# Two layer norms as pipelines of four stages in a fixed order, with other products between their last transposes

## The chip, the cores and the metric

The kernel runs on one core of a Trainium2 chip. The metric is the device time of one execution in microseconds. A core has five engines with queues of their own: TensorE (PE; its weight loads are PEld), VectorE (DVE), ScalarE (ACT), GpSimd (POOL) and SyncE (SP). Each engine takes its instructions in a fixed order and waits on semaphores for what others make. TensorE reads SBUF and writes banks of PSUM.

## The reference

One layer of a streaming encoder on 1024 frames of 1024 features, all in float32:

```
h = LN1(ALPHA * x + 0.5 * swiglu(x, ffn1_w1, ffn1_w3, ffn1_w2))
proj = h @ w_in                      # RWKV-7 time mixing, latent attention, two gates
mix  = (g_rwkv * y_rwkv + g_mla * y_mla) @ w_o
h = LN2(ALPHA * h + mix)
h = LN3(ALPHA * h + 0.5 * swiglu(h, ffn2_w1, ffn2_w3, ffn2_w2))

def layer_norm(x, g, b):
    mu = mean(x); var = mean((x - mu) ** 2)
    return (x - mu) * rsqrt(var + 1e-5) * g + b
swiglu(x, w1, w3, w2) = (silu(x @ w1) * (x @ w3)) @ w2
```

## The kernel before

Frames lie in eight tiles of 128 rows. Every matrix product is made of three products of a high and a low part (`mm3`, lines 240 to 243), so an operand is split into `h` and `l` first (`hilo`, line 250: the high part by ScalarE, the rest by VectorE or GpSimd at line 247; `split`, lines 1204 to 1210).

`ffn` (line 629) runs a feed-forward part. Weights come in pairs of tiles, and a pair is done by a Strassen-like scheme: seven products of sums of weight blocks with sums of blocks of x. `w_a` and `w_s` (lines 396 and 408) load weights and make the sums `rs`, `rt` and their parts `sh`, `sl`, `th`, `tl`; `XOps` (line 271) makes the blocks `b11`, `b21`, `b22` and the sums `t1` to `t4` of x. `Start` (line 429) handles the first three pairs; their first products (`p1`, `p2`) need no sums of weights.

`block` (line 568) makes the product that ends each of the three parts, in groups of rows of the second matrix: for every group all eight tiles get their products and are added into `acc` by VectorE. In the last group `ln_tile` (line 660) follows each tile: the sum over a row comes with the last addition (line 604), `nm` is the negative mean (667), ScalarE squares and sums (669), GpSimd makes the scalars `rs` and `nb` (674, 675, 684). Then the first and second norm have two ways. Tiles 0 to 5: ScalarE normalizes into `z` (685), GpSimd multiplies by the gain (686), VectorE adds the bias (687). Tiles 6 and 7, and all of the third norm: two VectorE operations (672, 678). In the first two norms the tile is then transposed by TensorE (695), eight blocks of 128x128 in two banks, and split by `sink.put` (lines 266 and 285: `HT` for the first norm, `XOps` for the second) into the operands of the next part.

The order is made by a scheduler when the program is built. It takes the instructions as written and lays each engine's queue by costs of its own; what stands in the queue then is fixed. After the first norm comes `mid` (line 1215), whose first job multiplies two tiles of `w_in` by the transposed tiles (`first`, line 1376). `BETWEEN` (line 457) says after which tile of the second norm a first product of a pair may come.

Buffers come in rings: `wraw` has 4 for raw weights, `wsp` 6 and `wsp2` 8 for split ones, `xp` 4 and `xf` 3 large ones; eight banks of PSUM are shared in four rings of two.

## Time and profile before

| | us |
|---|---|
| median of 3 runs (lowest, highest) | 2444.42 (2440.49, 2445.41) |
| profiled execution, its own time | 2448.22 |
| its span in the trace | 2446.3 |
| TensorE busy | 2317.0 (95%) |
| VectorE busy | 1503.5 (61%) |
| ScalarE busy | 797.6 (33%) |
| GpSimd busy | 649.2 (27%) |

The profiled execution's time is its span and 1.9 us around it. Busy times of matmuls overlap by their pipeline: one is shown 0.39 us long at the high clock, and the next starts 0.23 us after it. In the rows, an arrow in brackets gives how long an engine had been idle before an instruction and what released it. "PEclk" is the share of full clock that TensorE was granted in a stretch.

### The profile page before, as it was taken

To read this page: it belongs to the slowest core of one execution; us is meant where nothing else is said; L and a number is where in the kernel's file an instruction comes from. 1 tells how busy PE (TensorE), PEld (TensorE's weight loads), DVE (VectorE), ACT (ScalarE), POOL (GpSimd) and SP (SyncE) were. 2 spreads that over 40 slices of the span, in tenths; PEclk is the share of its full clock that TensorE was granted. 3 is DMA by queue.
4 is the path that set the end of the run, shared out by engine and by line. 5 is a ranking of instruction groups with operands and counts; after the bars stand their busy time and mean duration, and the time that the engine had idled before them with its cause. 6 is when DMAs were issued, how large, how long until landed. Compare 5 with 4: busy or idle time off the path is not lost.

```text
span 2446.3 us, 32472 instructions
## 1 busy us (share of the span) xinstructions
PE 2317.0 (95%) x12670; PEld 1902.9 (78%) x12670; DVE 1503.5 (61%) x2328; ACT 797.6 (33%) x1183; POOL 649.2 (27%) x559
## 2 busy tenths in 40 slices
PE   9999999999989998999999799889689999999998
PEld 7888888888768777877777588767468888888886
DVE  7866655666536546445373667766696666556666
ACT  5332223211353222222222566732442222231111
POOL 1322223322412003030122533343532222232311
PEclk9999999999989999999989999999799999999999
DMA  5322224532123313225226744463132222245311
GB/s 177 117 86 86 87 78 146 195 104 63 72 97 123 95 70 95 70 82 138 73 91 218 256 130 119 160 229 113 69 107 92 91 82 86 78 152 180 112 39 69
DMA packets 106265, 276.71 MB, mean 113 GB/s; under 512 B 36408, under 2 KB 36536, under 8 KB 106112
## 3 DMA queue, kind: packets, MB, share of 16 engines
q1 hardware_dynamic: 72912, 200.63, 24.1%
q0 software_dynamic: 19824, 71.38, 9.4%
q10 hardware_dynamic: 13376, 2.62, 0.7%
q8 instruction: 100, 1.64, 0.3%
q14 instruction: 53, 0.43, 0.1%
HBM read 193.98 MB, written 80.61 MB: 112 GB/s over the span
## 4 chain that ended last, share of the span: by engine, by line
PE 77%; DVE 7%; DMA 6%; issue 3%; POOL 3%; ACT 3%; SPq 0%; ACTq 0%; DVEq 0%; POOLq 0%
PE pd L241 5%; PE pd L242 5%; PE pd L243 5%; PE bb L242 4%; PE bb L241 4%; PE bb L243 4%; PE ba L241 4%; PE ba L242 4%; PE ba L243 4%; PE bc L243 4%; PE bc L242 4%; PE bc L241 4%; PE bd L243 4%; PE bd L242 4%; PE bd L241 4%
## 5 line engine op out<-in xcount | busy, mean ns | idle before, releaser
L241 PE MATMUL pd<-xh,wh 128*128 128x512 f32 x576 | 237.8, 413 | 1.7 <-DVE xl L1208 1.7
L242 PE MATMUL pd<-xl,wh 128*128 128x512 f32 x576 | 227.7, 395 | 0.0
L243 PE MATMUL pd<-xh,wl 128*128 128x512 f32 x576 | 227.5, 395 | 0.0
L247 POOL TENSOR_TENSOR la<-ra,ha 128x1024 fp32r<-128x1024 f32 x40 | 98.2, 2455 | 331.8 <-ACT ha L251 331.5
L241 PEld LDWEIGHTS pd<-xh,wh 128*128 128x128 f32 x576 | 109.9, 191 | 28.0 <-DVE xl L1208 1.9
L243 PEld LDWEIGHTS pd<-xh,wl 128*128 128x128 f32 x576 | 110.0, 191 | 24.4
L242 PEld LDWEIGHTS pd<-xl,wh 128*128 128x128 f32 x576 | 110.1, 191 | 21.6 <-issue 1.0
L251 ACT CAST ha<-ra 128x1024 fp32r<-128x1024 f32 (+1 forms) x45 | 46.4, 1033 | 245.4 <-PE bb L242 61.2
L247 POOL TENSOR_TENSOR fx<-raw,fx 128x1024 fp32r<-128x1024 f32 (+1 forms) x24 | 64.3, 2693 | 202.6 <-ACT fx L251 190.9
L247 POOL TENSOR_TENSOR wl<-raw,wh 128x1024 fp32r<-128x1024 f32 x28 | 73.0, 2610 | 140.1 <-ACT wh L251 121.5
L251 ACT CAST fx<-raw 128x1024 fp32r<-128x1024 f32 x44 | 44.1, 1049 | 158.2 <-DVE acc L607 47.6
L247 DVE TENSOR_TENSOR tl<-rt,th 128x1024 fp32r<-128x1024 f32 x41 | 85.5, 2086 | 0.0
L225 ACT CAST wh<-raw 128x1024 fp32r<-128x1024 f32 x36 | 37.7, 1048 | 145.9 <-PE pd L242 84.7
L247 POOL TENSOR_TENSOR hb<-rb,hb 128x512 fp32r<-128x512 f32 x41 | 56.9, 1387 | 85.8 <-ACT hb L251 85.7
L226 DVE TENSOR_TENSOR wl<-raw,wh 128x1024 fp32r<-128x1024 f32 x36 | 46.4, 1288 | 48.2 <-ACT wh L225 39.3
L222 POOL DMA_DIRECT2D raw<-in_w_in_dram x36 | 19.8, 550 | 201.1 <-DVE wl L226 80.7
L1666 ACT ACTIVATE pe<-s,anm,qs 128x512 f32<-128x512 f32 (+2 forms) x96 | 63.9, 670 | 25.2 <-DVE anm L1660 12.3
L607 DVE TENSOR_TENSOR acc<-acc,bd 128x512 f32<-128x512 f32 x72 | 49.3, 684 | 35.1 <-PE bd L243 34.9
L607 DVE TENSOR_TENSOR acc<-acc,ba 128x512 f32<-128x512 f32 x72 | 49.3, 684 | 34.9 <-PE ba L243 34.9
L1672 POOL TENSOR_SCALAR pe<-pe,asum 128x128 f32<-128x128 f32 (+3 forms) x64 | 47.7, 747 | 82.5 <-DVE asum L1671 76.7
L607 DVE TENSOR_TENSOR acc<-acc,bc 128x512 f32<-128x512 f32 x72 | 49.2, 684 | 32.2 <-PE bc L243 32.2
L607 DVE TENSOR_TENSOR acc<-acc,bb 128x512 f32<-128x512 f32 x72 | 49.2, 684 | 31.6 <-PE bb L243 31.4
(671 smaller groups left out, 6981.0 us busy)
## 6 DMA issues: line engine op xcount, KB each, us to landing
ra<-in_ffn_w_dram POOLq DMA_DIRECT2D x49, 512.0 KB, 3.7
raw<-in_ffn_w_dram SPq DMA_DIRECT2D x44, 512.0 KB, 4.2
raw<-gd_ffn SPq DMA_DIRECT2D x42, 512.0 KB, 4.4
rb<-in_ffn_w_dram POOLq DMA_DIRECT2D x41, 512.0 KB, 4.6
gd_ffn<-g SPq DMA_DIRECT2D x41, 512.0 KB, 2.6
raw<-in_w_in_dram POOLq DMA_DIRECT2D x36, 512.0 KB, 3.8
h<-acc SPq DMA_DIRECT2D x16, 512.0 KB, 2.6
gates<-dt SPq DMA_DIRECT2D x16, 512.0 KB, 3.3
```

The costliest lines, as they stand in the source:

```text
L222: (nc.gpsimd if K.pq else nc.sync).dma_start(out=raw[:rows, :n], in_=src)
L225: nc.scalar.copy(out=hi[:rows, :n], in_=raw[:rows, :n])
L226: nc.vector.tensor_tensor(out=lo[:rows, :n], in0=raw[:rows, :n], in1=hi[:rows, :n].bitcast(F32), op=ALU.subtract)
L241: nc.tensor.matmul(out, lhsT=lh, rhs=rh, start=start, stop=False)
L242: nc.tensor.matmul(out, lhsT=lh, rhs=rl, start=False, stop=False)
L243: nc.tensor.matmul(out, lhsT=ll, rhs=rh, start=False, stop=stop)
L247: eng.tensor_tensor(out=out, in0=a, in1=b, op=ALU.subtract)
L251: K.nc.scalar.copy(out=hi, in_=raw)
L607: nc.vector.tensor_tensor(out=at[:, ns], in0=at[:, ns], in1=ps, op=ALU.add)
L1666: nc.scalar.activation(out=pe[:, b:b + w], in_=s[:, 0:w], func=AF.Exp, scale=qs, bias=nm, accum_out=sm2[:, i:i + 1])
L1672: nc.gpsimd.tensor_scalar(out=pe[:, 0:n], in0=pe[:, 0:n], scalar1=sm_, scalar2=1.0, op0=ALU.mult, op1=ALU.mult)
```

## The change

In the first and second norm the last group becomes a loop of eleven steps inside a region in which the scheduler leaves TensorE, VectorE and GpSimd in the order in which the code is written. Step t makes the products and scalars of tile t, the gain of tile t-1 on GpSimd, the bias of tile t-2 on VectorE, and the transposes of tile t-3. All tiles go this way, in place in `acc`. After steps 8 and 9 of the first norm stand the first halves of the two products of `first`, whose weights are now loaded by SyncE's queue before the norm (class `Pre`); their results wait in two `raw` buffers. In the second norm two of the six first products stand after each of the steps 7, 8 and 9, then the sums of the first pair's weights, whose raw tiles are loaded earlier; the last sums of x (`X.end`) and those of the second pair come after the last subtraction of `put`. The last feed-forward part gets other groups: nine pairs and a last group of four. The third norm keeps its way.

```diff
@@ block
-        if final:
-            ln_tile(K, t, at, su, gb, sink, emit_h)
-            if between:
-                between(t)
+            hooks.weights()
+            sink.begin()
+            junk = K.tmp.tile([P, D], F32, name="junk", tag="r", bufs=2)
+            E = mybir.EngineType
+            with K.tc.manual_schedule(engines={E.PE, E.DVE, E.Pool}):
+                for t in range(NT + 3):
+                    if t < NT:
+                        ln_norm(K, at(t), last(t, at(t), ops), junk)
+                    if 1 <= t <= NT:
+                        nc.gpsimd.tensor_tensor(out=at(t - 1), in0=at(t - 1), in1=gb[0], op=ALU.mult)
+                    if 2 <= t < NT + 2:
+                        ln_out(K, t - 2, at(t - 2), gb, emit_h)
+                    if t >= 3:
+                        turn(K, t - 3, at(t - 3), sink)
+                    hooks.step(t)
@@ new functions
+def ln_norm(K, y, su, junk):
+    nc = K.nc
+    nm = ln_mean(K, su)
+    rs = ln_scale(K, y, nm, junk)
+    nb = K.small.tile([P, 1], F32, name="nb")
+    nc.gpsimd.tensor_tensor(out=nb, in0=rs, in1=nm, op=ALU.mult)
+    nc.scalar.activation(out=y, in_=y, func=AF.Identity, scale=rs, bias=nb)
+def ln_out(K, t, y, gb, emit_h):
+    K.nc.vector.tensor_tensor(out=y, in0=y, in1=gb[1], op=ALU.add)
+    emit_h(t, y, slice(0, D))
+class Pre:
+    def weights(self):
+        K = self.K
+        self.w = [load_w(K, K.a["w_in"][i]) for i in range(2)]
+        self.raw = [rawtile(K, "pre") for _ in range(2)]
+    def step(self, t):
+        if t not in (NT, NT + 1):
+            return
...
+            mm3(K.nc, ps, w[0][:, ks], w[1][:, ks], xs[k][0][:, 0:HALF], xs[k][1][:, 0:HALF], k == 0, k == KT - 1)
+        K.nc.scalar.copy(out=self.raw[i][:, 0:HALF], in_=ps)
@@ Start
+        if not self.w0:
+            self.raws = [w_raw(self.K, self.w13, self.first, n) for n in ("ra", "rb")]
...
+        if t == NT + 1:
+            self.sums(self.first, *self.raws)
...
+        with self.K.tc.issue_after(self.X.last.ins):
+            self.X.end()
+            self.sums(self.first + 1)
-BETWEEN = (0, 0, 0, 0, 1, 1, 1, 0)
+BETWEEN = (0, 0, 0, 0, 0, 0, 0, 2, 2, 2, 0)
@@ groups
-GROUPS = [(2 * i, 2 * i + 1) for i in range(8)] + [(16, 17, 18), (19, 20, 21)]
+_PAIRS = [(2 * i, 2 * i + 1) for i in range(9)]
+GROUPS = (_PAIRS[:8] + [(16, 17, 18), (19, 20, 21)], _PAIRS + [(18, 19, 20, 21)])
@@ mid
-    fill.add([lambda: load_w(K, a["w_in"][0]), lambda: load_w(K, a["w_in"][1])], first)
+    def first():
+        for w, raw, consume in zip(K.pre.w, K.pre.raw, (c_wa, c_g0)):
+            ps = K.pd.tile([P, S], F32, name="pd", tag="pd")
...
+            nc.scalar.copy(out=raw[:, HALF:S], in_=ps[:, HALF:S])
+            consume(raw)
```

What this does to the queues, at the three places where it matters. TensorE's queue at the end of the first norm, before (`ident,acc` is a group of four transposes, `fx` and `wh,gh` are operands of the last group, `xh,wh` of `first`):

```order
L695 MATMUL bd<-ident,acc 128x128 x4
L695 MATMUL ba<-ident,acc 128x128 x4
L596 MATMUL bc<-fx 128x512
L597 MATMUL bc<-fx 128x512
L695 MATMUL bd<-ident,acc 128x128 x4
L695 MATMUL ba<-ident,acc 128x128 x4
...
L241 MATMUL pd<-xh,wh 128x512
L242 MATMUL pd<-xl,wh 128x512
L243 MATMUL pd<-xh,wl 128x512
```

and in the changed kernel, where the rows left out are the rest of the 24 products after each tile:

```order
L749 MATMUL bd<-ident,acc 128x128 x4
L749 MATMUL ba<-ident,acc 128x128 x4
L242 MATMUL bb<-xh,wh 128x512
L243 MATMUL bb<-xl,wh 128x512
L244 MATMUL bb<-xh,wl 128x512
...
L749 MATMUL bc<-ident,acc 128x128 x4
L749 MATMUL bd<-ident,acc 128x128 x4
L242 MATMUL ba<-xh,wh 128x512
...
L749 MATMUL bb<-ident,acc 128x128 x4
L749 MATMUL bc<-ident,acc 128x128 x4
```

Before, the last four tiles were transposed one after another with no product between; now 24 products stand after each of tiles 5 and 6, and tile 7 comes last.

GpSimd's queue in the second norm, before (`rs` and `nb` are a tile's scalars, `z<-z,lngb` is the gain, `la` and `t` are splits):

```order
L247 TENSOR_TENSOR t_14352<-r_14354,t_14352 128x4x128
L674 TENSOR_SCALAR rs<-sq 128x1
L675 TENSOR_TENSOR rs<-rs,neghalf 128x1
L684 TENSOR_TENSOR nb<-rs,nm 128x1
L686 TENSOR_TENSOR z<-z,lngb 128x1024
L247 TENSOR_TENSOR t_14352<-r_14427,t_14352 128x4x128
```

and in the changed kernel:

```order
L248 TENSOR_TENSOR la<-ra,ha 128x1024
L710 TENSOR_SCALAR rs<-sq 128x1
L711 TENSOR_TENSOR rs<-rs,neghalf 128x1
L720 TENSOR_TENSOR nb<-rs,nm 128x1
L632 TENSOR_TENSOR acc<-acc,lngb 128x1024
L710 TENSOR_SCALAR rs<-sq 128x1
L711 TENSOR_TENSOR rs<-rs,neghalf 128x1
L720 TENSOR_TENSOR nb<-rs,nm 128x1
L632 TENSOR_TENSOR acc<-acc,lngb 128x1024
L248 TENSOR_TENSOR t_14445<-r_14447,t_14445 128x4x128
L632 TENSOR_TENSOR acc<-acc,lngb 128x1024
```

Before, a tile's gain stood right behind its own scalars; now the gain behind a tile's scalars is that of the tile before.

VectorE's queue at the end of the second norm, before (`t_14363` is the low part of `t2`, `t_14135` that of `t3`, `r_14591` belongs to `t4`, `s_` are sums of first products):

```order
L247 TENSOR_TENSOR tl<-rt,th 128x1024
L247 TENSOR_TENSOR r_14578<-bd,r_14569 128x512
L247 TENSOR_TENSOR r_14568<-bd,r_14568 128x512
L485 TENSOR_TENSOR s_14637<-cp,ba 128x512
L485 TENSOR_TENSOR s_14653<-cp,bb 128x512
L485 TENSOR_TENSOR s_14669<-cp,bc 128x512
L247 TENSOR_TENSOR t_14363<-r_14578,t_14363 128x4x128
L247 TENSOR_TENSOR r_14591<-b_14133,t_14363 128x1024
L247 TENSOR_TENSOR r_14597<-b_14133,t_14363 128x1024
L247 TENSOR_TENSOR b_14134<-bd,b_14134 128x4x128
L247 TENSOR_TENSOR t_14135<-r_14568,t_14135 128x4x128
```

and in the changed kernel:

```order
L423 TENSOR_TENSOR rs<-rb 128x512
L248 TENSOR_TENSOR rs<-rs,ra 128x512
L248 TENSOR_TENSOR rt<-ra,rb 128x512
L248 TENSOR_TENSOR rt<-ra,rs 128x512
L248 TENSOR_TENSOR sl<-rs,sh 128x1024
L248 TENSOR_TENSOR tl<-rt,th 128x1024
L248 TENSOR_TENSOR r_14641<-bd,b_14142 128x512
...
L248 TENSOR_TENSOR t_14145<-r_14640,t_14145 128x4x128
L314 TENSOR_TENSOR t_14456<-r_14650,t_14456 128x4x128
L248 TENSOR_TENSOR r_14664<-b_14143,t_14456 128x1024
```

Before, the sums of the first two pairs were mixed with the splits of the tiles; now the first pair's stand just ahead of the splits of tile 7, and the second pair's come after them. From the end of the first norm's products to the second norm TensorE's queue holds the same products in the same order in both.

## Rows read from the trace of the kernel before

**Rows 1.** Busy time by engine in two stretches; then clock, DMA share, GB/s.
```profile
633.80:697.50 63.70, 49.94 (x231) 41.20 (x230) 36.64 (x69) 28.82 (x44) 30.20 (x39) 0.87 0.19 71
1701.60:1805.20 103.60, 69.51 (x272) 53.64 (x273) 79.79 (x116) 47.88 (x72) 52.03 (x48) 0.82 0.26 92
```
**Rows 2.** Timeline of TensorE, first norm: start, duration, instruction, idle before.
```profile
633.87 0.39 PE L241 MATMUL bb<-wh,gh 128*128 128x512 f32 x1
...
651.11 0.60 PE L695 MATMUL bd<-ident,acc 128*128 128x128 f32 x4
651.54 0.60 PE L695 MATMUL ba<-ident,acc 128*128 128x128 f32 x4
...
678.68 1.09 PE L695 MATMUL bd<-ident,acc 128*128 128x128 f32 x4 [6.74 <-DVE acc L687]
...
686.31 0.80 PE L241 MATMUL pd<-xh,wh 128*128 128x512 f32 x1 [1.68 <-DVE xl L1208]
...
691.60 0.63 PE L241 MATMUL pd<-xh,wh 128*128 128x512 f32 x1
...
692.39 0.39 PE L243 MATMUL pd<-xh,wl 128*128 128x512 f32 x1
692.62 0.39 PE L241 MATMUL pd<-xh,wh 128*128 128x512 f32 x1
```
**Rows 3.** Timeline of TensorE, second norm and the start of the next part.
```profile
1742.99 1.09 PE L695 MATMUL bd<-ident,acc 128*128 128x128 f32 x4 [6.71 <-DVE acc L687]
...
1766.07 1.12 PE L695 MATMUL ba<-ident,acc 128*128 128x128 f32 x4 [8.77 <-DVE acc L687]
...
1805.26 0.39 PE L242 MATMUL bd<-t,sh 128*128 128x512 f32 x1
```
**Rows 4.** Timeline of all engines, the first tile of the first norm.
```profile
637.70 0.69 DVE L604 SCALAR_TENSOR_TENSOR acc<-acc,bc 128x512 f32<-128x512 f32 x1 [1.12 <-PE bc L597]
...
640.01 0.19 POOL L674 TENSOR_SCALAR rs<-sq 128x1 f32<-128x1 f32 x1 [24.04 <-ACT z L669]
...
641.15 1.24 ACT L685 ACTIVATE z<-acc,nb,rs 128x1024 f32<-128x1024 f32 x1 [1.23 <-POOL nb L684]
...
642.47 2.40 POOL L686 TENSOR_TENSOR z<-z,lngb 128x1024 f32<-128x1024 f32 x1 [1.36 <-ACT z L685]
```
**Rows 5.** Timelines of VectorE and GpSimd, two places of the first norm.
```profile
650.63 1.23 DVE L687 TENSOR_TENSOR acc<-z,lngb 128x1024 f32<-128x1024 f32 x1 [1.10 <-POOL z L686]
650.68 1.22 POOL L674 TENSOR_SCALAR rs<-sq 128x1 f32<-128x1 f32 x1
...
672.77 2.35 POOL L686 TENSOR_TENSOR z<-z,lngb 128x1024 f32<-128x1024 f32 x1
673.07 3.13 DVE L672 SCALAR_TENSOR_TENSOR c<-acc,nm,lngb 128x1024 f32<-128x1024 f32 x1 [0.22 <-ACT z L669]
```
**Rows 6.** Timeline of GpSimd: first of the constants' fills, then the second norm.
```profile
669.34 0.10 POOL L705 MEMSET hsel<- 128x2 f32 x1
...
1721.07 0.19 POOL L674 TENSOR_SCALAR rs<-sq 128x1 f32<-128x1 f32 x1
...
1756.49 1.29 POOL L247 TENSOR_TENSOR t<-r,t 128x512 fp32r<-128x512 f32 x1 [7.33 <-ACT t L251]
...
1774.80 2.76 POOL L247 TENSOR_TENSOR la<-ra,ha 128x1024 fp32r<-128x1024 f32 x1 [0.23 <-PE ba L242]
```
**Rows 7.** Timeline of VectorE, second norm: a short subtraction and a long one.
```profile
1793.80 0.68 DVE L247 TENSOR_TENSOR r<-bc,b 128x512 f32<-128x512 f32 x1
1794.40 1.21 DVE L247 TENSOR_TENSOR sl<-rs,sh 128x1024 fp32r<-128x1024 f32 x1
```
**Rows 8.** Timeline of TensorE and VectorE, end of the third norm.
```profile
2435.27 0.39 PE L597 MATMUL bd<-fx 128*128 128x512 f32 x1
...
2436.52 0.68 DVE L604 SCALAR_TENSOR_TENSOR acc<-acc,bd 128x512 f32<-128x512 f32 x1
...
2438.33 0.20 DVE L667 TENSOR_SCALAR nm<-su 128x1 f32<-128x1 f32 x1
...
2441.90 1.41 DVE L678 SCALAR_TENSOR_TENSOR acc<-c,rs,lngb 128x512 f32<-128x512 f32 x2 [0.71 <-POOL rs L675]
```

More of the change, by code (lines that the diff above doesn't have):

```diff
@@ L178, in body @@
                   lambda t, h, ns: nc.sync.dma_start(out=K.h2[t][:, ns], in_=h[:, ns]), X,
-                  before_last=st.weights, between=st.step)
+                  hooks=st)
             ffn(K, "ffn2", "ln3", X, st, resid=lambda t: K.h2[t],
@@ L311, in put @@
         hilo(K, self.r1, f("t1", 0), f("t1", 1), nc.gpsimd)
-        hilo(K, r2, f("t2", 0), f("t2", 1), nc.vector)
+        nc.scalar.copy(out=f("t2", 0), in_=r2)
+        self.last = nc.vector.tensor_tensor(out=f("t2", 1), in0=r2, in1=r("t2", 0), op=ALU.subtract)
     def end(self):
@@ L444, in step, with sums @@
             self.todo.pop(0)()
+        if t == NT + 1:
+            self.sums(self.first, *self.raws)
+    def sums(self, p, *raws):
+        w_s(self.K, self.w13, p, self.pairs[p].w, *raws)
     def run(self):
@@ L541, in tiles @@
         K = self.K
-        if (final and i == 2) or (not final and gi in (1, 2, 4, 6, 8)):
-            t = (K.xf if final else K.xp).tile([P, 4, S], F32R, name="fx", tag="x")
+        if (final and i >= 2) or (not final and gi in (1, 2, 4, 6, 8)):
+            t = (K.xf if final and i == 2 else K.xp).tile([P, 4, S], F32R, name="fx", tag="x")
             return [t[:, q] for q in range(4)]
@@ L565, in one, with block, mult, last @@
         return gh, None, wh, wl
-def block(K, src, groups, ln, resid, emit_h, sink, before_last=None, between=None):
+def block(K, src, groups, ln, resid, emit_h, sink, hooks=None):
     nc = K.nc
     acc = None
-    last = sink is None
+    tsl = lambda t: slice(t * P, (t + 1) * P)
+    def mult(t, ns, ops):
+        ps = bank(K)
+        for q, (gh, gl, wh, wl) in enumerate(ops):
+            st, sp = q == 0, q == len(ops) - 1
+            if gl is not None:
+                mm3(nc, ps, gh[:, tsl(t)], gl[:, tsl(t)], wh[:, ns], wl[:, ns], st, sp)
+            else:
+                nc.tensor.matmul(ps, lhsT=gh[:, tsl(t)], rhs=wh[:, ns], start=st, stop=False)
+                nc.tensor.matmul(ps, lhsT=gh[:, tsl(t)], rhs=wl[:, ns], start=False, stop=sp)
+        return ps
+    def last(t, at, ops):
+        su = K.small.tile([P, 2], F32, name="su")
+        for n, ns in halves():
+            ps = mult(t, ns, ops)
+            nc.vector.scalar_tensor_tensor(out=at[:, ns], in0=at[:, ns], scalar=1.0, in1=ps,
+                                           op0=ALU.mult, op1=ALU.add, accum_out=su[:, n:n + 1])
+        return su
     for gi, fs in enumerate(groups):
@@ L635, in ffn @@
         if nxt in st.pairs:
-            w_s(K, w13, nxt, st.pairs[nxt].w)
+            if not getattr(st.pairs[nxt], "summed", False):
+                st.sums(nxt)
         else:
@@ L675, in ln_tile @@
     nc.gpsimd.tensor_tensor(out=rs, in0=rs, in1=K.neghalf[:, 0:1], op=ALU.pow)
-    if fast:
-        for n, ns in halves():
-            nc.vector.scalar_tensor_tensor(out=y[:, ns], in0=c[:, ns], scalar=rs, in1=gb[1][:, ns],
-                                           op0=ALU.mult, op1=ALU.add)
-            if not transpose and t == NT - 1:
-                emit_h(t, y, ns)
-    else:
-        nb = sm.tile([P, 1], F32, name="nb")
-        nc.gpsimd.tensor_tensor(out=nb, in0=rs, in1=nm, op=ALU.mult)
-        nc.scalar.activation(out=z, in_=y, func=AF.Identity, scale=rs, bias=nb)
-        nc.gpsimd.tensor_tensor(out=z, in0=z, in1=gb[0], op=ALU.mult)
-        nc.vector.tensor_tensor(out=y, in0=z, in1=gb[1], op=ALU.add)
@@ L883 @@
 LAG = 2
-LNF = 6
 LA = 2
```

128 lines of the change are left out of this document (65 added, 63 removed).

## The prediction

> **What bounds the kernel now.** I read the page's busy shares first: TensorE is busy for 95% of the span, so over most of it only fewer products would help, and the change removes none. Next I cut the span at the places the diff touches. Around the first norm's last tiles, 63.7 us hold 49.94 us of TensorE work at a mean clock of 0.87; around the second norm 103.6 us hold 69.51 us at 0.82, and part of that busy time is itself stretched by the low clock [rows 1]. Everywhere else TensorE is nearly full. So the prize is what TensorE loses in these two stretches, and a little at the end.
>
> The third view is TensorE's timeline in the first of them. The last group's products start at 633.87. Then TensorE waits for normalized tiles, 6.74 us the longest time, and 1.68 us for the last split; the first product of the next section starts at 686.31, at the low clock (1.2 GHz, 0.63 us a product there), and the pace of the high one (2.4 GHz), 0.23 us from product to product, is back at 692.39 [rows 2]. In the second norm the same waits are 6.71 us and 8.77 us, and the dense stream of the next feed-forward part is there at 1805.26 [rows 3].
>
> The fourth view is one tile's way through the engines [rows 4]: VectorE adds the last product (637.70) and makes the mean, ScalarE squares, GpSimd makes the scalars from 640.01, ScalarE normalizes from 641.15, GpSimd multiplies by the gain (642.47, 2.40 us), and VectorE adds the bias. Some 9 us pass from the last product to a tile that can be transposed, against 3.63 us of products for a tile (16 of 0.227 us). The scheduler lets TensorE run out of products before these ways are over.
>
> **The change, part by part.** Eight tiles go through a fixed pipeline: at step t TensorE multiplies tile t, GpSimd makes its scalars and then multiplies tile t-1 by the gain, VectorE adds the bias to tile t-2, and TensorE transposes tile t-3. All eight tiles now take the GpSimd multiply; before, two of eight had a VectorE route. Products that need only earlier tiles stand between the last transposes: 48 in the first norm (the first half of two input projections), 72 in the second (first products of three pairs, which the scheduler had placed there partly).
>
> *The pace.* A GpSimd step is 1.11 us of scalars (640.01 to about 641.12) and 2.40 us of multiply, 3.5 us. But the trace shows that a VectorE operation with both inputs in SBUF and a GpSimd operation don't run side by side: a 0.19 us scalar takes 1.22 us beside the bias addition at 650.63, and VectorE's operation at 673.07, on as many elements as the bias addition, takes 3.13 us beside a GpSimd multiply that began at 672.77 [rows 4, 5]. Each step has one bias addition of 1.14 us (1.23 us in the row, less the overlap with the next). So I take 2.40 + 1.11 + 1.14 = 4.65 us a step. VectorE's own work in a step is 1.46 us for the additions and the mean, 1.14 us for the bias and 1.2 us for splits, 3.8 us; TensorE's is 3.63 + 0.86 us in the first norm and 2.72 + 0.86 us in the second.
> The Trainium skill ("SBUF — State Buffer", section "Who interferes with whom") calls the port pair that the two engines share an exclusive lock, so that whichever starts first blocks the other for its whole instruction; the rows just named agree. If the two merely ran beside each other, the step would be 3.5 us, and both norms would go by the first rival below.
>
> *First norm.* GpSimd's first multiply is now queued behind the second tile's scalars. Tile 1's scalars come 3.63 us after tile 0's (640.01), from 643.6 to 644.7 [rows 4]; so the multiply of tile 0 ends at 647.1, and, with tile 2's scalars held up by the first bias addition, that of tile 1 at 651.7. Four steps of 4.65 us later, at 670.3, tile 5 is multiplied, and it can be transposed at 671.5. From there TensorE has three tiles to transpose (0.86 us each, two groups of four that start 0.43 us apart in [rows 2]) and 48 products (10.9 us): 13.5 us, to 685.0. The fills of constants that stand in GpSimd's queue (669.34 to 672.77, about 3 us [rows 5, 6]) delay the last two multiplies to some 680; their transposes wait behind products anyway, so I cost them at nothing; without those products they would cost the 3 us. Then the 1.7 us for the last split, as before, and 2 us for a low clock after the wait at tile 5 (686.31 to 692.39 lost 2.9 us to it): the next products start near 689. Before, 48 products later than 686.31 is 692.39 plus the remaining 34 of 0.227 us, 700.1. Gain 11 us. Bounds: TensorE without any wait would be there at 633.87 + 128 x 0.227 + 6.9 + 10.9 + 1.7 = 682.5, a gain of 17.6 us; steps of 6.5 us would gain nothing.
> The halves computed early go through a copy by ScalarE before they are shifted, and two of four staging buffers are held until then. The copies lie beside the next 24 products, and weights loaded late have over 20 us until they are needed; I take 0, with bounds of -1 and +2 us.
>
> *Second norm.* GpSimd's first scalars are at 1721.07 [rows 6], behind two weight subtractions that stay there. Two tiles' scalars and the first multiply end at about 1725.9. Four steps bring tile 4 to 1744.5, a third weight subtraction in the queue (2.76 us) and two more steps tile 6 to 1756.6, and a split of 1.29 us with the last multiply tile 7 to 1760.3 [rows 6]. Here VectorE becomes the chain: a late tile's split is seven operations of 0.60 us [rows 7], 4.2 us, because these tiles feed the sums of a Strassen product. After the bias of tile 6 come the splits of tiles 5, 6 and 7 (12.6 us), three additions for the early products (1.8 us), the bias of tile 7 (1.14 us), the sums of the first pair's weights (4 of 0.60 and 2 of 1.21 us, 4.8 us), 20.3 us, and some 2 us of waits against GpSimd: 1782.6. TensorE has its last transposes behind it at about 1768 and then waits some 15 us, because all that is left needs tile 7. With 2 us of low clock it is dense as from 1785. Before, it was dense at 1805.26 with 16 products of that part done [rows 3], 3.6 us, which is 1801.6. The second pair's sums now stand behind the last subtraction (t4) on VectorE; they end some 15 us later, about when TensorE wants them; 1.5 us for that. Gain 15 us. Bounds: VectorE alone, never waiting, needs 49 us from the first addition, some 3 us before GpSimd's first scalars, which gives 1767 and a gain of 33 us; at the other end the wait eats all of it, 0 us or a loss as in the third rival.
>
> *Last norm.* The last group has four blocks of rows in place of three, so a tile has 22 products, 5.0 us, and VectorE, 4.3 us a tile, no longer falls behind. Now the last product starts at 2435.27 and its addition at 2436.52, the last mean follows only at 2438.33, after the tile before, and the last scaling at 2441.90 [rows 8]. Without the backlog the addition starts 0.4 us after the product does, the mean 0.7 us later, and the scaling 2.5 us after that (the way of [rows 4] up to the scalars): 2438.9. Gain 3 us, bounds 0 and 3.5.
>
> *Sum.* 11 + 15 + 3 = 29 us. The profiled execution took 2448.22 us (span 2446.3), so its like would take 2419; the runs' median is 2444.42, 3.8 us lower, so I predict 2415 us.
>
> **Rivals.** First, the queues never wait: the bias additions fit between GpSimd's operations. Then 17.6 + 33 + 3 = 54 us, 2390 us. For it: TensorE's and VectorE's own work would allow it. Against it: the blocked operations of [rows 5] are the rule when both engines are at work.
> Second, the wait only moves: in the second norm the 15 us at the end grow by what is saved between, because VectorE has the same splits and sums in any order; 11 + 0 + 3 = 14 us, 2430 us. For it: VectorE is busy 79.79 of the 103.6 us there [rows 1]. Against it: its busy time there holds blocked operations too (as the 3.13 us of [rows 5]), and those fixed queues may spare.
> Third, slower: with fixed queues one late tile holds all that is queued behind it, the stages stop overlapping, and the step grows to a tile's own way from the addition of its last product to the end of its bias addition, 8.4 us (637.70 to 644.87 and 1.23 us, [rows 4, 5]). The 29 us shrink by 12 for each us of the step (six steps in each norm), so 7.0 us a step decides; at 8.4 us it is 16 us slower, 2461 us. For it: the multiply of a tile waits for the scalars of the next. Against it: the multiply, the bias and the transposes belong to three different tiles.
> Fourth, the order changes nothing that can be measured: 2444 us. It would need steps near 7 us.
>
> **Numbers.** The forecast has 62%, its own range 2403 to 2428; the first rival 9%, the second 17%, the third 7%, the fourth 5%. The range that should hold the time 8 times in 10 takes in most of the second rival and goes part of the way to the first: 2400 to 2436. About 0.2% (4.9 us) is what a measurement can tell from no change; that gives 0.89 faster, 0.05 the same, 0.06 slower.
>
> **What would show it.** Right: in the first norm GpSimd's multiplies start 4.3 to 5 us apart, TensorE's one long wait is before the transposes of tile 5, and none stands before the last ones; in the second, TensorE waits once for 10 to 17 us after its last transposes, until VectorE's last split; at the end the last mean directly follows the last addition. Wrong: multiplies 3.5 us apart (first rival), a final wait over 25 us (second), steps of 7 us and more (third), or a loss in the sections between, where TensorE's order is the same as before.

## The result and the profile after

The changed kernel takes 2411.18 us (median of 4 runs, 2408.89 to 2413.39), the kernel before in the same session 2443.59: the ratio is 0.9874, with a 95% interval from 0.9859 to 0.9890, 32 us faster at the medians. The forecast was 2415. The profiled executions are 2413.39 us (span 2411.5) and 2448.22 us (span 2446.3), each longer than its median; their spans differ by 34.8 us.

To see where these 34.8 us lie, the span is cut at instructions that TensorE runs in both kernels: the first product `pr` behind the first norm, the first and the last product with `ym` (the part ahead of the second norm), the first product of the second down projection, the very last product. In the changed kernel they are:

```profile
704.36 0.47 PE L937 MATMUL pr<-x,w 128*128 128x512 f32 x1 [1.08 <-issue]
...
1572.37 0.50 PE L242 MATMUL bd<-ym,wu 128*128 128x512 f32 x1 [2.51 <-ACT wu L252]
...
1693.35 0.39 PE L244 MATMUL bc<-ym,wu 128*128 128x512 f32 x1
...
2166.48 0.39 PE L242 MATMUL bc<-wh,gh 128*128 128x512 f32 x1
...
2403.00 0.39 PE L600 MATMUL bb<-fx 128*128 128x512 f32 x1
```

and in the kernel before, where the last one, at 2435.27, is in [rows 8]:

```profile
713.53 0.47 PE L862 MATMUL pr<-x,w 128*128 128x512 f32 x1 [1.03 <-issue]
...
1584.42 0.49 PE L241 MATMUL bb<-ym,wu 128*128 128x512 f32 x1 [2.51 <-ACT wu L251]
...
1710.42 0.39 PE L243 MATMUL ba<-ym,wu 128*128 128x512 f32 x1
...
2198.76 0.39 PE L241 MATMUL ba<-wh,gh 128*128 128x512 f32 x1
```

Subtracting neighbours gives the length of each part.

| Part, us | before | after | gain |
|---|---|---|---|
| start to `pr` (holds the first norm) | 713.53 | 704.36 | 9.2 |
| `pr` to first `ym` (no edit here) | 870.89 | 868.01 | 2.9 |
| first to last `ym` (no edit here) | 126.00 | 120.98 | 5.0 |
| last `ym` to down projection (holds the second norm) | 488.34 | 473.13 | 15.2 |
| down projection to last product | 236.51 | 236.52 | 0.0 |
| last product to the end (last norm) | 11.0 | 8.5 | 2.5 |

In the `ym` part TensorE's order is not the same in both kernels, though the section on the change says so. Between the two marks it makes 492 products before and 483 in the changed kernel, where nine products with `wh` or `wl` have moved behind the last `ym`. These windows end just ahead of the next product, before first:

```profile
1584.42:1710.65 126.23, 116.99 (x492) 93.26 (x492) 76.08 (x93) 35.24 (x38) 48.27 (x26) 0.97 0.51 184
1572.37:1693.58 121.21, 114.19 (x483) 91.04 (x483) 72.58 (x93) 35.15 (x38) 49.22 (x26) 0.99 0.53 191
```

Nine products are 2.0 us at 0.227 us each. So 2.0 us of the 5.0 belong to the next part, which gained 17.2 us on the same products. The other 3.0 us are 2.2 us of TensorE's idle time (9.24 and 7.02 us) and 0.8 us of busy time, at a mean clock of 0.97 before and 0.99 after.

The last group of the first part begins at 635.35 in the changed kernel and at 633.87 before [rows 2], so the first norm itself gained 9.2 + 1.5 = 10.7 us. Two windows set beside [rows 1], from about the same place of the program to about the same place (columns as there), say how:

```profile
635.20:693.40 58.20, 52.43 (x254) 42.80 (x253) 35.41 (x66) 31.60 (x48) 32.50 (x46) 0.97 0.25 89
1684.70:1772.20 87.50, 62.62 (x269) 48.60 (x270) 68.14 (x105) 47.40 (x71) 53.71 (x49) 0.86 0.27 97
```

The first norm's window holds more TensorE work than before, in less time, at a clock of 0.97 in place of 0.87. TensorE's timeline there has one long wait, ahead of the transposes of tile 5, and answers to [rows 2]:

```profile
672.72 0.86 PE L749 MATMUL bd<-ident,acc 128*128 128x128 f32 x4 [3.37 <-DVE acc L725]
...
681.68 0.63 PE L749 MATMUL bc<-ident,acc 128*128 128x128 f32 x4 [0.79 <-DVE acc L725]
...
688.09 0.60 PE L749 MATMUL bb<-ident,acc 128*128 128x128 f32 x4
...
690.74 0.50 PE L242 MATMUL pd<-xh,wh 128*128 128x512 f32 x1 [1.61 <-DVE xl L1282]
```

The 0.79 us ahead of tile 6's transposes is short and none stands before tile 7's (688.09); behind the last 1.61 us wait TensorE stays at the high level (a granted clock of 1.00 from 690.74 to 697). GpSimd's gain multiplies (L632) set the pace of both norms; here are two of them and the scalar between, answering to [rows 4, 5]:

```profile
664.46 2.42 POOL L632 TENSOR_TENSOR acc<-acc,lngb 128x1024 f32<-128x1024 f32 x1
667.97 0.22 POOL L710 TENSOR_SCALAR rs<-sq 128x1 f32<-128x1 f32 x1 [1.09 <-ACT junk L708]
...
669.05 2.36 POOL L632 TENSOR_TENSOR acc<-acc,lngb 128x1024 f32<-128x1024 f32 x1
```

They start 4.6 us apart; in the kernel before, tiles 0 and 5 were multiplied at 642.47 and 672.77 [rows 4, 5], on the mean 6.1 us a step. In the first steps of a norm GpSimd goes as the forecast's sum has it: the scalar is held for 1.14 us (648.74) and 1.22 us (1709.60). But in the later steps GpSimd is idle for 1.1 us, waiting for ScalarE's square; that is not what the sum says, and several experiments are on it. In the second norm all engines show this end, answering to [rows 3, 7]:

```profile
1752.64 0.63 PE L749 MATMUL bd<-ident,acc 128*128 128x128 f32 x4 [0.55 <-DVE acc L725]
...
1763.80 0.68 DVE L248 TENSOR_TENSOR r<-bd,b 128x512 f32<-128x512 f32 x1
1764.51 1.04 DVE L248 TENSOR_TENSOR r<-r,b 128x512 f32<-128x512 f32 x1
1765.58 0.62 ACT L252 CAST t<-r 128x512 fp32r<-128x512 f32 x1 [2.44 <-DVE r L248]
...
1766.25 0.79 PE L242 MATMUL bd<-t,sh 128*128 128x512 f32 x1 [12.54 <-ACT t L252]
...
1768.85 0.68 DVE L314 TENSOR_TENSOR t<-r,t 128x512 fp32r<-128x512 f32 x1
...
1772.31 0.39 PE L242 MATMUL bb<-b,th 128*128 128x512 f32 x1
```

TensorE waits 12.54 us behind its last transposes, until VectorE comes to the splits of tile 7 and ScalarE makes the first cast from them. VectorE's last split starts 2.6 us after TensorE has gone on. The products come 0.43 us apart until 1772.04, the lower level (1.2 GHz, a granted clock of 0.51 in that stretch), and 0.23 us apart from 1772.31.

At the end of the kernel the addition, the mean and the last scalings follow the last product (2403.00) without a backlog; VectorE's rows answer to [rows 8]:

```profile
2403.43 0.69 DVE L607 SCALAR_TENSOR_TENSOR acc<-acc,bb 128x512 f32<-128x512 f32 x1 [0.33 <-PE bb L600]
...
2404.16 0.21 DVE L701 TENSOR_SCALAR nm<-su 128x1 f32<-128x1 f32 x1
...
2406.67 1.41 DVE L736 SCALAR_TENSOR_TENSOR acc<-c,rs,lngb 128x512 f32<-128x512 f32 x2 [0.98 <-POOL rs L711]
```

### The profile page after: what moved, and what is told of

It reads as the page before. It is cut to its first block, busy times and chain, and to the rows that moved or that the text cites. A ratio compares the mean times of both kernels' runs of the same rounds, so it can differ in the third digit from the quotient of the medians.

```text
span 2411.5 us, 32464 instructions
## 1 busy us (share of the span) xinstructions
PE 2303.4 (96%) x12670; PEld 1891.3 (78%) x12670; DVE 1491.9 (62%) x2320; ACT 803.3 (33%) x1191; POOL 653.2 (27%) x565
## 4 chain that ended last, share of the span: by engine, by line
PE 80%; DVE 5%; DMA 5%; ACT 3%; issue 3%; POOL 3%; SPq 0%; ACTq 0%; DVEq 0%; POOLq 0%
PE pd L242 6%; PE pd L243 5%; PE pd L244 5%; PE ba L242 5%; PE ba L243 5%; PE ba L244 5%; PE bb L243 4%; PE bb L242 4%; PE bb L244 4%; PE bd L243 4%; PE bd L242 4%; PE bd L244 4%; PE bc L243 4%; PE bc L242 4%; PE bc L244 4%
## 5 line engine op out<-in xcount | busy, mean ns | idle before, releaser
L242 PE MATMUL pd<-xh,wh 128*128 128x512 f32 x560 | 230.1, 411 | 1.6 <-DVE xl L1282 1.6
L244 PE MATMUL pd<-xh,wl 128*128 128x512 f32 x560 | 220.4, 394 | 0.0
L243 PE MATMUL pd<-xl,wh 128*128 128x512 f32 x560 | 220.3, 393 | 0.0
L248 POOL TENSOR_TENSOR la<-ra,ha 128x1024 fp32r<-128x1024 f32 x40 | 96.9, 2424 | 325.4 <-ACT ha L252 325.4
```

Source lines behind the costliest of these rows:

```text
L242: nc.tensor.matmul(out, lhsT=lh, rhs=rh, start=start, stop=False)
L243: nc.tensor.matmul(out, lhsT=lh, rhs=rl, start=False, stop=False)
L244: nc.tensor.matmul(out, lhsT=ll, rhs=rh, start=False, stop=stop)
L248: eng.tensor_tensor(out=out, in0=a, in1=b, op=ALU.subtract)
```

## The experiments

Two of the parts, `pr` to `ym` and `ym`, differ from profile to profile by more than some of the effects looked for, and each kernel has one profile. A norm is therefore read from the part that holds it, in the profile of each kernel; the whole time stands beside it, with its ratio to runs of the kernel before on the same chip (95% interval; their medians were 2444.71 us for a1 to a4, 2442.72 for a5 to a8, 2440.20 for a9 to a11 and 2437.95 for a12).

| Kernel | us, median | ratio | to `pr` | `pr` to `ym` | `ym` | second norm | end |
|---|---|---|---|---|---|---|---|
| before | 2443.59 | 1 | 713.5 | 870.9 | 126.0 | 488.3 | 11.0 |
| changed | 2411.18 | 0.9874 (0.9859 to 0.9890) | 704.4 | 868.0 | 121.0 | 473.1 | 8.5 |
| a1 | 2413.41 | 0.9877 (0.9862 to 0.9891) | 703.6 | 863.3 | 121.9 | 474.5 | 11.5 |
| a2 | 2426.13 | 0.9929 (0.9917 to 0.9941) | 702.8 | 864.7 | 120.8 | 491.0 | 8.5 |
| a3 | 2424.43 | 0.9921 (0.9906 to 0.9936) | 711.8 | 861.9 | 125.0 | 472.5 | 8.1 |
| a4 | 2423.88 | 0.9917 (0.9905 to 0.9930) | 712.8 | 862.4 | 124.3 | 473.6 | 8.5 |
| a5 | 2419.36 | 0.9908 (0.9894 to 0.9922) | 706.1 | 865.7 | 124.1 | 477.8 | 8.5 |
| a6 | 2408.54 | 0.9863 (0.9848 to 0.9877) | 702.6 | 865.7 | 121.0 | 473.2 | 8.5 |
| a7 | 2411.63 | 0.9877 (0.9862 to 0.9892) | 703.6 | 862.5 | 123.6 | 473.5 | 8.5 |
| a8 | 2428.23 | 0.9947 (0.9932 to 0.9962) | 711.8 | 862.7 | 126.5 | 479.5 | 8.5 |
| a9 | 2393.98 | 0.9811 (0.9796 to 0.9826) | 697.1 | 863.9 | 122.2 | 462.5 | 8.5 |
| a10 | 2415.21 | 0.9895 (0.9880 to 0.9910) | 703.4 | 861.7 | 123.4 | 478.8 | 8.4 |
| a11 | 2413.17 | 0.9884 (0.9867 to 0.9902) | 703.4 | 867.8 | 123.1 | 477.8 | 8.9 |
| a12 | 2412.30 | 0.9892 (0.9872 to 0.9911) | 704.7 | 862.3 | 122.6 | 472.6 | 8.5 |

The part left out, down projection to last product, takes 236.3 to 238.6 us. Kernels with the changed first norm as it is (the changed kernel, a1, a2, a7, a10 to a12) lie from 702.8 to 704.7 us, those with the changed second norm as it is (a1, a3, a4, a12 and the changed kernel) from 472.5 to 474.5 us: differences under 2 us in these columns show nothing. The `ym` part holds 492 products before and in a2, 483 in the others, and the second norm's part nine fewer in these two.

**One part undone at a time.** a1, the last feed-forward part's groups as before:

```diff
-GROUPS = (_PAIRS[:8] + [(16, 17, 18), (19, 20, 21)], _PAIRS + [(18, 19, 20, 21)])
+GROUPS = (_PAIRS[:8] + [(16, 17, 18), (19, 20, 21)],) * 2
```

> The changed kernel with the last feed-forward part's groups as before: (16,17,18) and (19,20,21) in place of (16,17) and (18,19,20,21). Theory (the third term of the sum): in the last group a tile then has 16 products, 3.6 us, VectorE needs 4.3 us a tile and falls behind, the last mean follows the last addition by over 1 us again, and the kernel takes 2.5 to 3 us more than the changed one: 2414. Rival: the wait behind the last products is only moved to another place at the end, and the time stays at 2411 (within 0.5 us).

The end is 3.0 us longer (11.5 against 8.5 us), as the theory has it; the whole times are not told apart (0.9877 and 0.9874). VectorE's rows show the backlog back again: the last mean is made 1.8 us after its addition began, against 0.7 us above, with rows of the tile before in between.

```profile
2400.90 0.68 DVE L607 SCALAR_TENSOR_TENSOR acc<-acc,bb 128x512 f32<-128x512 f32 x1
...
2401.51 1.28 DVE L734 SCALAR_TENSOR_TENSOR c<-acc,nm,lngb 128x1024 f32<-128x1024 f32 x1
2402.71 0.20 DVE L701 TENSOR_SCALAR nm<-su 128x1 f32<-128x1 f32 x1
```

a2, the second norm as before (old `block` and `ln_tile` kept beside the new ones):

```diff
-            block(K, Mix(K, ym), ..., X, hooks=st)
+            block0(K, Mix(K, ym), ..., X, before_last=st.weights, between=st.step)
```

> The changed kernel with the second norm as before (scheduler's order, three early products put between tiles 4 to 6, sums of both pairs behind it). Theory: the second norm's term is worth 15 us, as the marks on TensorE's timeline give it (17.1 us ahead at the start of that norm's last group, 32.3 us ahead behind it), so 2426; the 7.9 us that the changed kernel gains between the end of the first norm and the start of the second one's last group stay, because they come from the first norm's shift or from chance. Rival 1: those 7.9 us come with the second norm's edits (the scheduler moves loads and VectorE's work in the groups ahead of it), and go too: 2431 to 2434. Rival 2: the terms overlap, and the second norm's order alone is worth less than 8 us: under 2419.

The second norm's part is 491.0 us, 17.9 us longer than with the change, with nine products fewer; the whole is 2426, as the theory says. The parts ahead of the norm keep their length (864.7 and 120.8 us), so rival 1 is out; 2426 is far over 2419, so rival 2 is out too.

a3, the first norm as before (old `block` for the first feed-forward part, `first` as before, no `Pre`):

```diff
-    block(K, Down(K, K.a[name + "_w2"]), GROUPS[sink is None], ln, resid, emit_h, sink, hooks)
+    (block if sink is None else block0)(K, Down(K, K.a[name + "_w2"]), GROUPS[sink is None], ln, resid, emit_h, sink)
```

> The changed kernel with the first norm as before (scheduler's order, all products of the input projections behind the transposes). Theory: the first norm's term is worth 9.2 us at the first mark behind it, so 2420 to 2421. Rival: the gain of 7.9 us between the norms hangs on the first norm's shift and goes with it: 2426 to 2429. If the three terms add up, the losses of this kernel, of the one with the second norm as before and of the one with the last group as before sum to 32 us; if not, something in between is shared.

The part to `pr` is 7.4 us longer and the `ym` part 4.0 us longer. The whole time, 2424, is between the two answers (the profiled execution, 2418.31 us, is the fastest of its six). Undoing the three parts one at a time costs 3.0 us (a1), 17.9 us (a2) and 7.4 us (a3), 28 us in all by the parts that hold them and 30 us by the medians, of the 32: the terms nearly add up.

a4, the pipeline of the first norm kept, but its early products back behind the transposes (`Pre.step` returns at once, `first` and the loading of its weights as before):

```diff
     def step(self, t):
-        if t not in (NT, NT + 1):
-            return
+        return
```

> The changed kernel with the first norm's pipeline kept, but without products between its last transposes: the first half of the two input projections is back behind the transposes, beside the second half. Theory: the pipeline alone hardly moves the end of the norm, because GpSimd's pace (4.6 us a step) sets when the last tile can be transposed; the gain is the 10.9 us of products that fill that wait. Without them TensorE waits about 4 us before each of the last two transposes, more with the 3 us of fills in GpSimd's queue, is at the low clock, and the first products of the next section start near 685 us with 48 more to do: 8 to 9 us more than the changed kernel, 2419 to 2420. Rival: the pipeline itself carries the gain (tiles come earlier than before), and the products' place is worth under 3 us: 2411 to 2414.

The part to `pr` is 712.8 us: 8.4 us longer than with the change, and nearly as long as before (713.5). GpSimd's pace is the same 4.6 us. TensorE's timeline shows the wait that the products filled, and the lower level (0.43 us a product, a granted clock of 0.50 from 681.3 to 690) behind it:

```profile
672.42 0.73 PE L749 MATMUL bd<-ident,acc 128*128 128x128 f32 x4 [3.37 <-DVE acc L725]
...
681.29 1.09 PE L749 MATMUL bb<-ident,acc 128*128 128x128 f32 x4 [7.28 <-DVE acc L725]
...
683.52 1.11 PE L749 MATMUL bd<-ident,acc 128*128 128x128 f32 x4 [0.30 <-DVE acc L725]
...
686.89 0.80 PE L242 MATMUL pd<-xh,wh 128*128 128x512 f32 x1 [1.40 <-DVE xl L1279]
```

In the kernel before, tile 5 is transposed at 678.68 [rows 2] and tile 7 at:

```profile
682.75 0.63 PE L695 MATMUL bd<-ident,acc 128*128 128x128 f32 x4 [0.49 <-DVE acc L678]
```

Counted from the last group's first product (635.03 in a4, 633.87 before), the pipeline alone brings tile 5 7.4 us earlier, but tile 7 only 0.4 us (48.5 and 48.9 us), and the part to `pr` is 1.9 us shorter. So at most 1.9 of the 10.7 us come with the pipeline alone, and the rest with what TensorE does while it waits for the last three tiles. These products need tiles 0 to 3 alone; what they would gain in the old order, without the pipeline, was not run.

**What sets the pace.** a5 exchanges two rows of a step:

```diff
-                    if 2 <= t < NT + 2:
-                        ln_out(K, t - 2, at(t - 2), gb, emit_h)
                     if t >= 3:
                         turn(K, t - 3, at(t - 3), sink)
+                    if 2 <= t < NT + 2:
+                        ln_out(K, t - 2, at(t - 2), gb, emit_h)
```

> The changed kernel with two rows of a step exchanged: VectorE splits tile t-3 ahead of the bias addition of tile t-2, not behind it. Theory 1 (as predicted): the pace of a step is a sum on GpSimd, 2.40 multiply + 1.11 scalars + 1.14 us in which the bias addition keeps it out; the order of VectorE's rows changes nothing, and the multiplies stay 4.6 us apart in both norms. Theory 2 (from the trace of the changed kernel, where GpSimd is idle for 1.1 us of each step, waiting for ScalarE's square): the pace is half of a loop over two steps, multiply, bias addition, two splits, two additions and mean of the next tile, square, scalars, multiply, 9.1 us; with the splits (1.2 us) out of it the loop is 7.9 us, and the multiplies come 4.0 us apart in the second norm (in the first TensorE's own 4.49 us a step keeps them at 4.5). The whole kernel: 2411 by theory 1, 2407 to 2410 by theory 2.

Both theories missed: the steps of the second norm grow to 5.16 us, and the second norm loses 4.7 us by the table (the first 1.8 us, hardly more than the spread). The timeline of VectorE, ScalarE and GpSimd in one step shows a loop that neither had:

```profile
1724.94 1.24 ACT L721 ACTIVATE acc<-acc,nb,rs 128x1024 f32<-128x1024 f32 x1 [1.81 <-POOL nb L720]
1726.09 0.57 ACT L1280 CAST b<-bd 128x512 fp32r<-128x512 f32 x1
...
1726.68 0.69 DVE L1282 TENSOR_TENSOR b<-bd,b 128x512 fp32r<-128x512 f32 x1 [1.27 <-ACT b L1280]
...
1727.89 1.22 DVE L725 TENSOR_TENSOR acc<-acc,lngb 128x1024 f32<-128x1024 f32 x1
1728.36 0.79 POOL L710 TENSOR_SCALAR rs<-sq 128x1 f32<-128x1 f32 x1 [1.11 <-ACT junk L708]
...
1730.02 2.40 POOL L632 TENSOR_TENSOR acc<-acc,lngb 128x1024 f32<-128x1024 f32 x1
```

The splits wait for ScalarE's cast, which stands behind ScalarE's normalization, which waits for GpSimd's scalars; and the bias addition, now behind the splits, runs when the next scalar is ready and stretches it to 0.79 us. Splits that wait hold up the addition behind them on VectorE. This account is read from the rows; no run tests it by itself.

a6 puts one more step between a tile's gain and its bias:

```diff
-                    if 2 <= t < NT + 2:
-                        ln_out(K, t - 2, at(t - 2), gb, emit_h)
-                    if t >= 3:
-                        turn(K, t - 3, at(t - 3), sink)
+                    if 3 <= t < NT + 3:
+                        ln_out(K, t - 3, at(t - 3), gb, emit_h)
+                    if t >= 4:
+                        turn(K, t - 4, at(t - 4), sink)
```

> The changed kernel with one more step between a tile's gain multiply and its bias addition and transposes (bias of tile t-3, transposes of tile t-4; the early products one step later too). Theory 1, the sum on GpSimd: the same operations exclude each other as before, and the multiplies stay 4.6 us apart. Theory 2, the loop: a multiply now waits for a bias addition three steps back, 9.1 us over three steps, which binds no longer; in the second norm the multiplies come 3.5 to 4.0 us apart, by VectorE's own 3.8 us of work, in the first 4.5 us by TensorE's. The whole kernel: 2411 to 2413 by theory 1, 2406 to 2410 by theory 2.

The multiplies of the second norm still come 4.57 us apart, and 4.4 to 4.6 in the first: theory 1's pace. GpSimd, which has no idle time now, and VectorE show why:

```profile
1716.76 2.41 POOL L632 TENSOR_TENSOR acc<-acc,lngb 128x1024 f32<-128x1024 f32 x1
...
1719.21 1.23 DVE L725 TENSOR_TENSOR acc<-acc,lngb 128x1024 f32<-128x1024 f32 x1 [0.69 <-POOL acc L632]
1719.26 1.23 POOL L710 TENSOR_SCALAR rs<-sq 128x1 f32<-128x1 f32 x1
...
1721.34 2.36 POOL L632 TENSOR_TENSOR acc<-acc,lngb 128x1024 f32<-128x1024 f32 x1
```

The scalar that takes 0.22 us above takes 1.23 us, exactly as long as the bias addition that began just ahead of it. The whole time, 2408.5, lies in theory 2's range, but its ratio (0.9863) is not told apart from that of the changed kernel; the pace decides between the theories.

a8 makes the square of each tile twice:

```diff
+    sq = K.small.tile([P, 1], F32, name="sq2")
+    nc.scalar.activation(out=junk, in_=y, func=AF.Square, bias=nm, accum_out=sq)
     rs = ln_scale(K, y, nm, junk)
```

> The changed kernel with ScalarE's square of each tile done twice in the first two norms (its result is not changed), 1.25 us more on the way from a tile's mean to its scalars, no work added on GpSimd or VectorE. Theory 1, the sum on GpSimd: the multiplies stay 4.6 us apart, since GpSimd's own work is the same and ScalarE has room; 2411 to 2413. Theory 2, the loop over two steps: it grows from 9.1 to 10.4 us, the multiplies come 5.2 us apart, the last one is about 4 us later in each norm; 2415 to 2419.

In the second norm the multiplies start at 1723.56, 1729.37, 1735.20 and 1740.06, 5.5 us apart on the mean, with GpSimd idle for 1.4 to 2.4 us of a step; 7.4 and 6.4 us are lost in the two norms. That is the direction of theory 2, and more than its 5.2 us and its 4 us a norm; the whole, 2428, is above its 2415 to 2419. Why the loop grew by more than the added square is open.

a9 is a6 without the bias additions:

```diff
-    K.nc.vector.tensor_tensor(out=y, in0=y, in1=gb[1], op=ALU.add)
```

> The kernel with one more step between gain and bias, without the bias additions of the first two norms (the bias is left out). Theory 1, VectorE's bias addition keeps GpSimd out: with it gone a step is 2.40 + 1.11 us on GpSimd, and in the second norm the multiplies come 3.5 to 3.7 us apart (TensorE's step is 3.58 us), and no scalar operation of GpSimd takes over 0.6 us. Rival: GpSimd's step of 4.57 us is its own (the scalar that takes 1.23 us is slow behind a multiply, whatever VectorE does): the multiplies stay 4.6 us apart. The whole kernel: in both theories some us less, since VectorE's queue at the end of the second norm is shorter by the additions too (3 x 1.14 us); 2398 to 2405 by theory 1, 2404 to 2408 by the rival.

The steps of the second norm fall to 3.53 us, and the scalar to 0.19 us:

```profile
1703.44 2.40 POOL L632 TENSOR_TENSOR acc<-acc,lngb 128x1024 f32<-128x1024 f32 x1
1705.92 0.19 POOL L710 TENSOR_SCALAR rs<-sq 128x1 f32<-128x1 f32 x1
...
1706.96 2.40 POOL L632 TENSOR_TENSOR acc<-acc,lngb 128x1024 f32<-128x1024 f32 x1
```

The whole, 2394, is under the 2398 to 2405 of theory 1: the forecast was too careful. 4.57 - 3.53 = 1.04 us of each step are the time for which VectorE's bias addition keeps GpSimd out. The Trainium skill ("SBUF — State Buffer", section "Who interferes with whom") says that a VectorE instruction with two inputs in SBUF contends with a GpSimd instruction that reads SBUF; these two kernels agree. With a6, a8 and a9 the pace has two causes that happen to be equally long in the changed kernel: the sum on GpSimd, 4.57 us (a6), and half of a loop through VectorE's queue and ScalarE, 9.1 us over two steps (GpSimd's 1.1 us of idle time, and a8). Taking away the loop alone (a6) gains nothing; the bias addition was not taken away with the loop left in place.

**What sets the wait of 12.5 us.** a10 does one row of the splits four times:

```diff
-        sub(nc.vector, r2, pt, self.r1)
+        for _ in range(4):
+            sub(nc.vector, r2, pt, self.r1)
```

> The changed kernel with one of the rows that split tiles 4 to 7 in the second norm (the one that makes r2) done four times in place of once: 1.8 us more VectorE work a tile, nothing else. Theory: VectorE's queue sets when TensorE goes on after the last transposes, so the three tiles split behind the last additions cost 5.4 us: from the last product ahead of the last group to the first product of the down projection the kernel takes 478 to 481 us in place of 473, and the whole 2416 to 2419. Rival: the wait of 12.5 us is set by another engine (ScalarE's casts or GpSimd's splits), VectorE has slack beside them: 473 to 475 us, and 2411 to 2413.

The second norm's part takes 478.8 us, 5.6 us more, for 5.4 us of work added to the three last tiles: VectorE's queue is the chain there. The whole, 2415.2, is not clear of the changed kernel's by its ratio. The wait is longer too:

```profile
1765.81 0.79 PE L242 MATMUL bd<-t,sh 128*128 128x512 f32 x1 [14.72 <-ACT t L252]
```

a7 puts the first pair's sums ahead of the splits of tile 5:

```diff
+                    if t == NT and hasattr(hooks, "raws"):
+                        hooks.sums(hooks.first, *hooks.raws)
                     if t >= 3:
                         turn(K, t - 3, at(t - 3), sink)
...
-        if t == NT + 1:
-            self.sums(self.first, *self.raws)
```

> The changed kernel with the sums of the first pair's weights one step earlier on VectorE: ahead of the splits of tile 5, not of those of tile 7. Theory: in the second norm VectorE's queue sets when TensorE may go on; it is idle there for 3.1 us in the splits of tile 5, and moving 4.8 us of sums ahead of them fills the wait for ScalarE; VectorE's last split comes 2 to 3 us earlier and so does the dense stream: 2408 to 2410. Rival: the sums delay the transposes of tiles 6 and 7 by as much as they spare later, and the wait of 12.5 us is only cut into two: 2411 to 2413.

The rival holds: the part is 473.5 us, the same, and the wait is cut in two, 5.67 us ahead of tile 7's transposes and 6.45 us behind them. The expectation placed VectorE's idle 3.1 us wrongly: it is in the splits of tile 4 (3.09 us in the changed kernel), ahead of the moved sums, and stays there (3.21 us); in those of tile 5 VectorE waits 0.8 us.

```profile
1754.43 1.09 PE L749 MATMUL bd<-ident,acc 128*128 128x128 f32 x4 [5.67 <-DVE acc L725]
1762.82 0.79 PE L242 MATMUL bd<-t,sh 128*128 128x512 f32 x1 [6.45 <-ACT t L252]
```

a11 gives a low half of the splits to GpSimd:

```diff
-        hilo(K, self.r12, f("t3", 0), f("t3", 1), nc.vector)
+        hilo(K, self.r12, f("t3", 0), f("t3", 1), nc.gpsimd)
```

> The changed kernel with the low half of t3 in the splits of tiles 4 to 7 made by GpSimd, which is idle there, in place of VectorE: 0.60 us a tile less on VectorE, 1.27 us more on GpSimd. Theory, the two engines exclude each other when VectorE's inputs are both in SBUF: VectorE is kept out for up to 1.27 us for each 0.60 us spared, so nothing is won and up to 2 us are lost: 2411 to 2414. Rival: GpSimd's work lies beside VectorE's waits for ScalarE (0.7 us in each of these splits, 3.1 us in that of tile 5) and the three tiles behind the last additions spare 1.8 us: 2409.

The part takes 4.7 us more in the profile, worse than the theory's 2 us and by another way. The profiled execution, 2420 us, is the slowest of its four; the median, 2413, lies in the theory's range and is not told apart from the changed kernel's. Two splits of tile 4, in place of one, now stand ahead of tile 7's multiply in GpSimd's queue and wait for ScalarE; that multiply starts 8.0 us behind the one before, not 3.6 us as in the changed kernel (1737.08 and 1740.68):

```profile
1738.34 2.41 POOL L632 TENSOR_TENSOR acc<-acc,lngb 128x1024 f32<-128x1024 f32 x1
1743.43 2.98 POOL L248 TENSOR_TENSOR t<-r,t 128x512 fp32r<-128x512 f32 x2 [2.68 <-ACT t L252]
1746.37 3.37 POOL L632 TENSOR_TENSOR acc<-acc,lngb 128x1024 f32<-128x1024 f32 x1
```

**The gain in the parts that were not changed.** a12 fixes VectorE's order in the first group of the `ym` part as the kernel before had it:

```diff
+        if gi == 0 and isinstance(src, Mix):
+            inorder.enter_context(K.tc.manual_schedule(engines={mybir.EngineType.DVE}))
+        if gi == 1:
+            inorder.close()
```

> The changed kernel, with VectorE's order fixed in the first group of the part ahead of the second norm: all sixteen residual additions before the gate products of the next group, as the scheduler had it in the kernel before (in the changed kernel it put one gate product two additions earlier, though nothing of the change stands there). Theory: the 5.0 us by which that part (from the first product with ym to the last) is shorter in the changed kernel, 121.0 against 126.0 us, is mostly this row: 124 to 126 us here, and 2414 to 2416 for the whole. Rival: the row's place is a sign and not a cause, and the part's length hangs on when the residuals land: about 121 us, and 2411 to 2413.

122.6 us: neither answer. In the other kernels the part takes 120.8 to 123.6 us where the scheduler put a gate product two additions earlier (the changed kernel, a1, a2, a6, a7, a9, a10, a11) and 124.1 to 126.5 us where it did not (before, a3, a4, a5, a8); a12, which did not by its edit, lies among the first. So the row goes along with the length but isn't shown to cause it. TensorE's idle time in a12, 9.3 us, is that of the kernel before (9.2), which would put the 2.2 us of idle time down to the row; but it is 8.6 and 9.0 us in a7 and a9 too, which have the row early. Of the 5.0 us the nine products are settled, the 2.2 us are open.

## Why the prediction was right, point by point

**Pace of a step.** Forecast 4.65 us as a sum on GpSimd; measured 4.57. a9 shows that the bias addition's share of the sum is real, a6 that the sum binds by itself. What the forecast did not have is the second limit of the same length: in the later steps of the changed kernel GpSimd waits for a square in the very time in which it would be kept out. That the pace came out as forecast in these steps too is luck: with a longer loop (a8) it is 5.5 us.

**First norm, 11 us.** Measured 10.7 us within the stage. Tile 5 is transposed at 672.72, 671.24 if the stage is counted from the same start; the forecast said 671.5. The first product of the next section comes at 690.74, 689.3 by that start, against "near 689". The fills of constants delay the next multiply by 2.1 us (steps of 6.65 and 4.57 us) and cost at most the 0.79 us ahead of tile 6's transposes, because products stand there: a4, without these products, waits 7.28 us in their place and has lost 8.4 us.

**Second norm, 15 us.** Measured 15.2 us. The kernel reaches this norm 17.1 us earlier than before (last `ym`), and with that added the steps are where the forecast had them: GpSimd's first scalars, at 1704.01 in the changed kernel, at 1721.1 (1721.07), TensorE going on at 1783.3 (1782.6). Two steps were wrong and made up for each other. VectorE's last split ends at 1769.53, 1786.6 on the forecast's count, 4 us later than its 1782.6: a tile's splits take 5.4 to 5.7 us, not 4.2, with 0.7 to 0.8 us of waiting for a cast by ScalarE in each. But TensorE does not wait for that last split; it waits for ScalarE's first cast of tile 7's splits, and three rows of VectorE start after it has gone on. The forecast's second rival, that the wait merely moves, is what a7 does to the wait, but not what the change did.

**Last norm, 3 us.** Measured 2.5 us at the end of the span, 3.0 us in a1. Addition 0.4 us after the last product, mean 0.7 us later, scaling 2.5 us after it: as forecast.

**The sum.** 10.7 + 15.2 + 2.5 = 28.4 us, against 29. The spans differ by 34.8 us; the other 6.4 us are -1.5 us ahead of the first norm (its last group begins at 633.3 to 635.7 us in the fourteen kernels), 2.9 us between `pr` and `ym` and 5.0 us in the `ym` part, where the forecast expected no change. Between `pr` and `ym` TensorE's order is the same, and TensorE's busy time alone is 4.0 us less (814.3 and 810.2 us). That part took 861.7 to 870.9 us in fourteen profiles of fourteen kernels, the kernel before the longest; that the 2.9 us are chance is likely, not shown. In the `ym` part 2.0 us are the nine products that moved into the second norm's part, 0.8 us busy time, 2.2 us open. So the forecast of 2415, 4 us too slow, had the sum of the change's own terms right, by errors that cancelled in the second norm, and nothing for these parts, which could as well have moved the whole some us the other way.

**Rivals.** The steps that never wait (2390) need the bias additions out of GpSimd's way: a9, which leaves the bias out, has them out and takes 2394. The steps did not grow to 7 us (6.7 us once in each norm, where fills or a weight subtraction stand in GpSimd's queue), and the end of the second norm kept its gain.

## What to carry to other kernels

In these pipelines the pace was the longest of three things: each engine's own work in a step, GpSimd's work plus VectorE's operations with both inputs in SBUF, and the loops that the in-order queues close, divided by the steps they span; work all three out before moving a row. Where the last tiles cannot come earlier, look for products that need only the early ones: in the first norm the kernel lost 8.4 us without them (a4). And read such a change from the parts that hold it, because the parts outside it moved by up to 9 us between profiles; count that two marks hold the same instructions before you subtract them.

## What the runs showed of the hardware that was not expected

Exchanging two VectorE rows that are not dependent on each other lengthened a step from 4.57 to 5.16 us (a5); by the rows, a row that waits holds back the one behind it. The part between `pr` and `ym` holds the same TensorE instructions in all kernels, yet TensorE's clock falls in it at different places: in a stretch with 149 products and transposes in both, the kernel before ran at a mean clock of 0.73 and the changed one at 0.93, and TensorE's busy time was 22.55 and 18.54 us. These are the two windows, before first:

```profile
1236.00:1263.00 27.00, 22.55 (x149) 19.39 (x150) 17.19 (x37) 6.44 (x10) 1.71 (x3) 0.73 0.30 87
```

```profile
1225.00:1250.00 25.00, 18.54 (x149) 15.03 (x151) 17.21 (x38) 6.25 (x10) 1.71 (x3) 0.93 0.33 93
```
